# Pinning three engines to the order of the source in an expert loop, with the index work drawn apart

## The chip, the core and the metric

The kernel runs on one core of a Trainium2 chip. The metric is the device time of one execution in microseconds; lower is better.

## What is computed

A decoder layer over 512 tokens of width 1024, in float32: a mixer of retention and differential attention, then an expert network of 32 experts, of which every token takes four, then a last norm. The change touches the expert network alone:

```python
def moe_ffn(h, w_router, b_router, w1, b1, w2, b2):
    ...
    top_v, top_i = lax.top_k(logits, TOP_K)
    gate = jax.nn.softmax(top_v, axis=-1)
    ...
    def expert_block(args):
        xb, e = args
        hid = xb @ w1[e] + b1[e]
        return swiglu_clamped(hid) @ w2[e] + b2[e]
    ...
    out = jax.ops.segment_sum(ys.astype(jnp.float32) * slot_w[:, None], slot_tok, num_segments=T)
```

w1 is 1024 x 2048 and w2 1024 x 1024 an expert: 12 MB of weights for each of 32 experts, all of which are read.

## The kernel before

**Weights.** A matrix product is made of three: each operand is split into a high and a low part in the fast matmul format, and `three()` (L520 to L523) adds high x high (L521), high x low (L522) and low x high (L523). The weights stream from memory in chunks of 1 MB (128 x 2048 floats, two pages of the 48 that `Pages` hands out), eight for w1 and four for w2 of an expert. SyncE issues the loads (L134). `Whole.make` converts a chunk: ScalarE writes the high part to a second pair of pages (L481), VectorE overwrites the raw chunk with the low part (L484); for the first experts GpSimd does some of the latter. When TensorE is through with a chunk, `done()` frees its four pages, `st.pump()` issues the next load into two of them and `cm.run()` converts the next chunk into two, as long as fewer than five converted chunks stand ready (`Whole(5)`). `st.keep` holds back pages; it is 12 from expert 29 on.

**The loop** (L1313 ff.) runs e from 0 to 32. Iteration e does w1 of expert e and then w2 of expert e - 1. `w1_start(e)` (L1109) lays the biases down in PSUM banks 0 to 3 by four matmuls. `w1_unit(e, u)` is one of 16 units of six matmuls; after each odd unit a chunk is done. After unit 2, `turn_hidden` transposes the hidden rows of expert e - 1 (L1099, eight transposes into banks 4 and 5), and ScalarE and VectorE take them out as two parts (L1087, L1088). Then come eight units of w2 into banks 6 and 7, six matmuls each, with a chunk done after each odd one. After unit 0 and unit 1 `swiglu` reads half of banks 0 to 3 (ScalarE L1127, VectorE L1128 and L1129); after unit 2 `turn` transposes the gathered rows of the next expert (L1092, then L1087 and L1088 again). `result(e - 1)` scales the product by the gate on ScalarE (L1205), and GpSimd adds its rows to y in memory by an indirect DMA (L1206).

**The index work.** `index(e)` writes a one-hot of 128 slots x 512 tokens on VectorE (OH, one buffer; L1064), multiplies it with a small table by four matmuls (L1068, bank 4), reads out the row numbers and the gate by three small VectorE instructions (L1069, L1071, L1072), and gathers the expert's rows from memory by GpSimd (L1080) into `Xg[e % 2]`. In iteration e it is called for expert e + 2 after unit 0 of w1. For the last two experts it also transposes the one-hot (L1077).

**The end.** The last two experts aren't scattered: `result_last` (L1150 to L1152) splits their rows, `combine` (L1160) adds them by matmuls, and `gather_sums` (L1168 to L1173), called after expert 29's result, loads the other input of the sum and the rows of y (GpSimd's queue, L1173). `add_sums(i)` (L1176, L1177) multiplies and adds them on VectorE, called after units 4 to 7 of w2 of expert 30. `finish` norms and stores.

**Order.** The source lists the instructions, but Tile's scheduler orders each engine's queue by its own model of when things are ready; data dependences hold in any order. `tc.keep_in_program_order(ins)` ties an instruction behind the one before it on its engine in the source. Before the change this is used in a few places only (`later_dma`, `first_rows`, the first conversions). At run time each engine takes its queue strictly in the order given.

Of the kernel before, what the change touches and what calls it, by code (L numbers as in the profile page):

```python
# [17 lines left out]
ALU = mybir.AluOpType  # L18
AX = mybir.AxisListType

P = 128
D = 1024
S = 512
NT = S // P
KT = D // P
E = 32
# [78 lines left out]
class Stream:  # L105
# [18 lines left out]
    def issue(self):  # L124
        src, n, shape = self.items[self.next]
        if shape is None:
            self.next += 1
            src()
            return
        b = Buf(self.mem, n)  # L130
        v = b.ap
        if len(shape) == 2:
            v = v.rearrange("p (a b) -> p a b", a=shape[0])
        self.nc.sync.dma_start(v, src)  # L134
        self.bufs[self.next] = b
        self.next += 1
# [51 lines left out]
    yield from b  # L188


@with_exitstack
def decoder_layer(ctx, tc, t, out):
    nc = tc.nc
    pe, dve, act, pool = nc.tensor, nc.vector, nc.scalar, nc.gpsimd
    cp = ctx.enter_context(tc.tile_pool(name="cp", bufs=1))
    pp = ctx.enter_context(tc.tile_pool(name="pp", bufs=1, space=bass.MemoryType.PSUM))
    dp = ctx.enter_context(tc.tile_pool(name="dp", bufs=1, space=bass.MemoryType.DRAM))
# [4 lines left out]
    def bank(b, n=1):  # L202
        return ps[:, b * 512:(b + n) * 512]
# [96 lines left out]
    iota1, tri, iota32, sel64 = cst[:, 0:128], cst[:, 128:256], cst[:, 256:288], cst[:, 288:352]  # L300
# [22 lines left out]
    def sm(name, shape, dt=F32):  # L323
        if name not in small:
            small[name] = cp.tile(shape, dt, name=name)
        return small[name]
# [98 lines left out]
    class Conv:  # L425
# [4 lines left out]
        def __init__(self, ahead):  # L430
            self.units, self.made, self.ahead, self.next, self.sub = [], {}, ahead, 0, dve
            self.pinned = False
# [425 lines left out]
    VAL = cp.tile([P, NT, E, 4], F32R, name="VAL")  # L858
    posm = cp.tile([P, NT, E], F32, name="posm")
# [42 lines left out]
    OH = cp.tile([P, NT, P], F32R, name="OH")  # L902
# [158 lines left out]

    def index(e):
        if e > 0:
            dve.tensor_tensor(OH, iota1.unsqueeze(1).to_broadcast([P, NT, P]),  # L1064
                              posm[:, :, e:e + 1].to_broadcast([P, NT, P]), op=ALU.is_equal)
        o = bank(4)[:, 0:4]
        for i in range(NT):
            pe.matmul(o, OH[:, i, :], VAL[:, i, e, :], start=(i == 0), stop=(i == NT - 1))  # L1068
        dve.tensor_tensor(idx[e % 6], o[:, 0:2], spare, op=ALU.add)  # L1069
        gs = sm("gs", [P, 2])  # L1070
        dve.tensor_copy(gs, o[:, 2:4])  # L1071
        dve.tensor_scalar(gate[e % 6], gs[:, 0:1], gs[:, 1:2], 1.0 / ALPHA, op0=ALU.add, op1=ALU.mult)  # L1072
        if e == 0:
            return
        if e >= E - LAST:
            for i in range(NT):
                pe.transpose(bank(5)[:, i * P:(i + 1) * P], OH[:, i, :].bitcast(F32), ident)  # L1077
            oht[e] = Buf(mem, 1).r[:, 0:512]
            act.activation(oht[e], bank(5), AF.Copy)
        pool.indirect_dma_start(out=Xg[e % 2].ap, out_offset=None, in_=h2_dram,  # L1080
                                in_offset=bass.IndirectOffsetOnAxis(ap=idx[e % 6][:, 0:1], axis=0),
                                bounds_check=S - 1, oob_is_err=False)

    def turned(b, hb, lb):
        for n in range(2):
            cs = slice(n * 512, (n + 1) * 512)
            act.activation(hb.r[:, cs], bank(b + n), AF.Copy)  # L1087
            dve.tensor_tensor(lb.r[:, cs], bank(b + n), hb.r[:, cs].bitcast(F32), op=ALU.subtract)  # L1088

    def turn(src, hb, lb):  # L1090
        for k in range(KT):
            pe.transpose(bank(4 + k // 4)[:, (k % 4) * P:(k % 4 + 1) * P], src[:, k * P:(k + 1) * P], ident)  # L1092
        turned(4, hb, lb)
# [12 lines left out]
    def w1_start(e):  # L1106
        for n in range(4):
            h = n // 2
            pe.matmul(bank(n), selr[:, h * E + e:h * E + e + 1].to_broadcast([P, P]),  # L1109
                      b12.r[:, n % 2 * 512:(n % 2 + 1) * 512], start=True, stop=False)  # L1110

    def w1_unit(e, u):
        k = u // 2
        wH, wL = cm.get(u1[e][k])
        xh, xl = parts(XH, XL, k)
        for n in range(2 * (u % 2), 2 * (u % 2) + 2):
            cs = slice(n * 512, (n + 1) * 512)
            three(bank(n), xh, xl, wH[:, cs], wL[:, cs], False, k == KT - 1)
        if u % 2:
            cm.done(u1[e][k])  # L1120
            cm.run()

    def swiglu(n, sg, ub):

        hid = bank(2 * n, 2).rearrange("p (f two) -> p f two", two=2)
        cs = slice(n * 512, (n + 1) * 512)
        act.activation(sg.ap[:, cs], hid[:, :, 0], AF.Silu, scale=ALPHA)  # L1127
        dve.tensor_scalar(ub.ap[:, cs], hid[:, :, 1], -LIMIT + 1.0, LIMIT + 1.0, op0=ALU.max, op1=ALU.min)  # L1128
        dve.scalar_tensor_tensor(sg.ap[:, cs], sg.ap[:, cs], SILU_MAX, ub.ap[:, cs], op0=ALU.min, op1=ALU.mult)  # L1129
# [45 lines left out]
    def add_sums(i):  # L1175
        dve.tensor_tensor(sums[i].ap, sums[i].ap, g2_row, op=ALU.mult)  # L1176
        dve.tensor_tensor(xt[i], xt[i], sums[i].ap, op=ALU.add)  # L1177
        sums[i].free()
# [134 lines left out]
    index(0)  # L1313
    index(1)
    for e in range(E + 1):
        if e < E:
            w1_start(e)
            if e == E - LAST - 1:
                st.keep = 12
            for u in range(16):  # L1320
                if e == 0 and u >= 13:
                    cm.sub = pool
                w1_unit(e, u)
                if u == 2 and e > 0:
                    turn_hidden(aH, aL)
                if u == 0 and e + 2 < E:
                    index(e + 2)
                if e == 0 and u == 3:
                    gates_turned()
                if e == 0 and u in (5, 7, 9, 11):  # L1330
                    first_sums((u - 5) // 2)
        if e > 0:
            for u in range(8):
                w2_unit(e - 1, u)
                if e < E and u in (0, 1):
                    swiglu(u, sg, ub)
                if u == 2 and e + 1 < E:
                    turn(Xg[(e + 1) % 2].ap, XH, XL)
                if u == 4 and e == E - 1:
                    turn_hidden(XH, XL)  # L1340
                if e == E - LAST + 1 and u >= 4:
                    add_sums(u - 4)
            if e - 1 >= E - LAST:
                result_last(e - 1)
            else:
                result(e - 1)
            if e == E - LAST:
                gather_sums()
        else:
            swiglu(0, sg, ub)  # L1350
            swiglu(1, sg, ub)
            count_extra()
            cm.sub = dve
            turn(Xg[1].ap, XH, XL)

    for b in [XH, XL, aH, aL, sg, ub, yb] + Xg:
        b.free()

# [121 lines left out]
```

## Time and profile before

| | us |
|---|---|
| median of 3 runs | 1585.27 (1583.05 to 1587.38) |
| the profiled execution, its own time | 1585.85 |
| its span, first to last instruction | 1584.0 |
| busy: TensorE / VectorE / ScalarE / GpSimd | 1473.3 / 1323.9 / 993.9 / 171.3 |

PE is TensorE, PEld its weight loads, DVE VectorE, ACT ScalarE, POOL GpSimd, SP SyncE. A matmul of 512 columns shows a duration of about 0.39 us, but the next one starts 0.23 us after it: for TensorE the distance from start to start counts. A wait is put down to what came last.

### The profile page before, as it was taken

The page shows a single profiled execution, that of the slowest core. Times are in us where ns is not written, and L with a number is a line of the kernel's source. Part 1 is how long each engine was busy: PE and PEld are TensorE (multiplying, and loading weights), DVE is VectorE, ACT ScalarE, POOL GpSimd, SP SyncE. Part 2 cuts the span into 40 slices and gives each one's busy share as a digit, 9 for nine tenths or more (in the row PEclk, how much of TensorE's full clock was granted, in tenths as well). Part 3 has the DMA queues.
Part 4 walks back from the last instruction along what each step waited for, and adds up shares of the span by engine and source line. Part 5 has one row for each costly group of instructions (what it writes and reads, how often), then busy time and mean ns, then how long its engine had stood idle before and what let it go on. Part 6 is the DMA issues. An engine that isn't in the chain of part 4 may idle for free.

```text
span 1584.0 us, 18643 instructions
## 1 busy us (share of the span) xinstructions
PE 1473.3 (93%) x6837; PEld 1195.5 (75%) x6837; DVE 1323.9 (84%) x1405; ACT 993.9 (63%) x917; POOL 171.3 (11%) x94
## 2 busy tenths in 40 slices
PE   3999999787999999999999999999999999999956
PEld 3787688766888888888777777777777777887744
DVE  6868767996999989888888888888888888888767
ACT  3525434466777777766666666666666666776724
POOL 0000000442000111111000000000000011110001
PEclk9999999988999999999999999999999999999978
DMA  9871473548999999999999999999999999987962
GB/s 364 314 272 30 157 266 134 198 180 312 353 363 363 372 356 358 369 364 359 351 345 346 345 348 334 354 336 342 346 340 339 345 346 349 349 321 277 329 246 81
DMA packets 88812, 485.19 MB, mean 306 GB/s; under 512 B 12433, under 2 KB 18996, under 8 KB 39182
## 3 DMA queue, kind: packets, MB, share of 16 engines
q1 hardware_dynamic: 75792, 453.54, 76.1%
q0 software_dynamic: 9360, 18.05, 4.5%
q10 hardware_dynamic: 3566, 12.37, 2.1%
q8 instruction: 56, 0.92, 0.2%
q14 instruction: 38, 0.31, 0.1%
HBM read 475.82 MB, written 25.44 MB: 316 GB/s over the span
## 4 chain that ended last, share of the span: by engine, by line
PE 58%; DVE 8%; ACT 5%; DMA 5%; issue 2%; POOL 1%; ACTq 0%; DVEq 0%; POOLq 0%
PE ps L522 19%; PE ps L523 18%; PE ps L521 16%; DVE part L484 6%; ACT part L481 5%; DMA page<-in_w_dram 3%; PE ps L1099 2%; PE ps L1092 1%; PE ps L1109 1%; DMA y_dram<-page,idx 1%; POOL part L484 1%; DMA page<-y_dram 1%; DVE page L1129 0%; DVE page L1368 0%; DMA page<-x_dram 0%
## 5 line engine op out<-in xcount | busy, mean ns | idle before, releaser
L484 DVE TENSOR_TENSOR part<-page,part 128x2048 fp32r<-128x2048 f32 x378 | 855.3, 2287 | 98.8 <-ACT part L481 96.6
L481 ACT ACTIVATE part<-page 128x2048 fp32r<-128x2048 f32 x384 | 718.8, 1912 | 80.9 <-PE ps L522 70.7
L522 PE MATMUL ps<-part,part 128*128 128x512 f32 x1792 | 721.6, 403 | 49.2 <-DVE part L484 41.9
L523 PE MATMUL ps<-part,part 128*128 128x512 f32 x1792 | 706.4, 394 | 3.5 <-DVE part L1088 3.5
L521 PE MATMUL ps<-part,part 128*128 128x512 f32 x1792 | 623.3, 396 | 3.3 <-ACT part L616 3.2
L522 PEld LDWEIGHTS ps<-part,part 128*128 128x128 f32 x1792 | 339.6, 190 | 137.4 <-DVE part L484 61.7
L521 PEld LDWEIGHTS ps<-part,part 128*128 128x128 f32 x1792 | 338.9, 189 | 78.4 <-issue 3.7
L523 PEld LDWEIGHTS ps<-part,part 128*128 128x128 f32 x1792 | 339.6, 190 | 73.0 <-DVE part L1088 4.2
L1087 ACT ACTIVATE part<-ps 128x512 fp32r<-128x512 f32 x128 | 74.1, 598 | 170.2 <-PE ps L1099 81.4
L1206 POOL DMA_INDIRECT y_dram<-page,idx x30 | 71.9, 2397 | 740.7 <-ACT page L1205 705.3
L1088 DVE TENSOR_TENSOR part<-ps,part 128x512 fp32r<-128x512 f32 x128 | 86.3, 684 | 38.0 <-ACT part L1087 38.0
L1127 ACT ACTIVATE page<-ps 128x512 f32<-128x512 f32 x64 | 37.6, 589 | 118.8 <-PE ps L523 118.8
L1080 POOL DMA_INDIRECT page<-h_dram,idx x31 | 47.6, 1534 | 282.7 <-DVE gs L1071 270.5
L1128 DVE TENSOR_SCALAR page<-ps 128x512 f32<-128x512 f32 x64 | 43.8, 687 | 22.0 <-ACT page L1127 21.9
L447 ACT ACTIVATE part<-page 128x1024 fp32r<-128x1024 f32 x32 | 33.5, 1055 | 26.4 <-DMA page<-in_w_in_dram 9.3
L450 DVE TENSOR_TENSOR part<-page,part 128x1024 fp32r<-128x1024 f32 x32 | 38.7, 1221 | 10.7 <-ACT part L447 10.5
L1129 DVE SCALAR_TENSOR_TENSOR page<-page,page 128x512 f32<-128x512 f32 x64 | 47.3, 746 | 0.0
L1109 PE MATMUL ps<-part,selr 128*128 128x512 f32 x128 | 40.8, 411 | 5.8 <-DVE page L1128 4.8
L420 DVE SCALAR_TENSOR_TENSOR page<-page,sc,page 128x1024 f32<-128x1024 f32 x32 | 40.9, 1280 | 5.3 <-DMA page<-in_w_ada_dram 4.9
L1099 PEld LDWEIGHTS ps<-ident,page 128*128 128x128 f32 x256 | 40.5, 202 | 5.1
L1205 ACT ACTIVATE page<-ps,gate 128x1024 f32<-128x1024 f32 x30 | 33.5, 1116 | 15.6 <-PE ps L523 15.6
L1099 PE MATMUL ps<-ident,page 128*128 128x128 f32 x256 | 41.8, 279 | 0.0
(219 smaller groups left out, 803.4 us busy)
## 6 DMA issues: line engine op xcount, KB each, us to landing
page<-in_w_dram SPq DMA_DIRECT2D x384, 1024.0 KB
page<-in_w_ada_dram SPq DMA_DIRECT2D x22, 1024.0 KB
page<-in_w_in_dram SPq DMA_DIRECT2D x12, 1024.0 KB
page<-in_w_out_dram SPq DMA_DIRECT2D x4, 1024.0 KB
page<-in_x_dram SPq DMA_DIRECT2D x4, 512.0 KB
page<-in_w_ada_dram SPq DMA_DIRECT2D x4, 512.0 KB
page<-in_x_dram SPq DMA_DIRECT2D x2, 1024.0 KB
x_dram<-page ACTq DMA_DIRECT2D x4, 512.0 KB
```

The lines of the kernel that those rows point to most:

```text
L481: ins = act.activation(h.r, b.ap, AF.Copy)
L484: ins = self.sub.tensor_tensor(b.r, b.ap, h.r.bitcast(F32), op=ALU.subtract)
L521: pe.matmul(o, aH, bH, start=first, stop=False)
L522: pe.matmul(o, aH, bL, start=False, stop=False)
L523: pe.matmul(o, aL, bH, start=False, stop=last)
L1080: pool.indirect_dma_start(out=Xg[e % 2].ap, out_offset=None, in_=h2_dram, in_offset=bass.IndirectOffsetOnAxis(ap=idx[e % 6][:, 0:1], axis= ...
L1087: act.activation(hb.r[:, cs], bank(b + n), AF.Copy)
L1088: dve.tensor_tensor(lb.r[:, cs], bank(b + n), hb.r[:, cs].bitcast(F32), op=ALU.subtract)
L1099: pe.transpose(bank(4 + k // 4)[:, (k % 4) * P:(k % 4 + 1) * P], src[:, k // 2, k % 2, :], ident)
L1109: pe.matmul(bank(n), selr[:, h * E + e:h * E + e + 1].to_broadcast([P, P]), b12.r[:, n % 2 * 512:(n % 2 + 1) * 512], start=True, stop=False)
L1129: dve.scalar_tensor_tensor(sg.ap[:, cs], sg.ap[:, cs], SILU_MAX, ub.ap[:, cs], op0=ALU.min, op1=ALU.mult)
L1206: pool.indirect_dma_start(out=y_dram, out_offset=bass.IndirectOffsetOnAxis(ap=idx[e % 6][:, 1:2], axis=0), in_=yb.ap, in_offset=None, boun ...
```

## The change

The three engines' handles are wrapped, so that each instruction issued through them while `pin` is set is tied behind the one before it on its engine. `pin` is set for TensorE, VectorE and ScalarE from iteration 1 to the end of the loop; GpSimd and SyncE are not wrapped. `index` is cut in three: `place` (the one-hot), `look_up` (the four matmuls) and `take_rows` (the rest). In iterations 1 to 29 `look_up(e + 2)` follows unit 8 of w1, `take_rows(e + 2)` unit 10, and `place(e + 3)` follows unit 0 of w2 and the first half of the SwiGLU. Expert 0's iteration still calls `index(2)` after unit 0, and ends with `place(3)`.

```diff
+class Engine:
+
+    def __init__(self, tc, engine):
+        self.tc, self.engine, self.pin = tc, engine, False
+
+    def __getattr__(self, name):
+        f = getattr(self.engine, name)
+
+        def issue(*args, **kw):
+            ins = f(*args, **kw)
+            return self.tc.keep_in_program_order(ins) if self.pin else ins
+
+        return issue
...
-    pe, dve, act, pool = nc.tensor, nc.vector, nc.scalar, nc.gpsimd
+    pe, dve, act, pool = Engine(tc, nc.tensor), Engine(tc, nc.vector), Engine(tc, nc.scalar), nc.gpsimd
...
     def index(e):
         if e > 0:
-            dve.tensor_tensor(OH, iota1.unsqueeze(1).to_broadcast([P, NT, P]),
-                              posm[:, :, e:e + 1].to_broadcast([P, NT, P]), op=ALU.is_equal)
+            place(e)
+        look_up(e)
+        take_rows(e)
+
+    def place(e):
+        dve.tensor_tensor(OH, iota1.unsqueeze(1).to_broadcast([P, NT, P]),
+                          posm[:, :, e:e + 1].to_broadcast([P, NT, P]), op=ALU.is_equal)
+
+    def look_up(e):
+        for i in range(NT):
+            pe.matmul(bank(4)[:, 0:4], OH[:, i, :], VAL[:, i, e, :], start=(i == 0), stop=(i == NT - 1))
+
+    def take_rows(e):
         o = bank(4)[:, 0:4]
-        for i in range(NT):
-            pe.matmul(o, OH[:, i, :], VAL[:, i, e, :], start=(i == 0), stop=(i == NT - 1))
         dve.tensor_tensor(idx[e % 6], o[:, 0:2], spare, op=ALU.add)
...
     for e in range(E + 1):
+        if e == 1:
+            pe.pin = dve.pin = act.pin = True
...
-                if u == 0 and e + 2 < E:
-                    index(e + 2)
+                if e == 0 and u == 0:
+                    index(2)
+                if 0 < e < E - 2:
+                    if u == 8:
+                        look_up(e + 2)
+                    if u == 10:
+                        take_rows(e + 2)
...
                 if e < E and u in (0, 1):
                     swiglu(u, sg, ub)
+                if u == 0 and e < E - 3:
+                    place(e + 3)
...
             turn(Xg[1].ap, XH, XL)
-
+            place(3)
+
+    pe.pin = dve.pin = act.pin = False
```

## Rows read from the trace of the kernel before

**Rows 1.** The page: its first line, and the granted TensorE clock in 40 slices of the span, in tenths of full speed.

```profile
span 1584.0 us, 18643 instructions
...
PEclk9999999988999999999999999999999999999978
```

**Rows 2.** The windows: stretch, its length, then the busy time (and the count of instructions) of PE, PEld, DVE, ACT and POOL, the granted clock, the DMA share, GB/s.

```profile
405.40:693.50 288.10, 288.10 (x1346) 240.12 (x1345) 257.48 (x191) 212.59 (x150) 31.78 (x16) 1.00 0.97 364
700.00:1400.00 700.00, 679.19 (x3101) 550.49 (x3101) 601.30 (x443) 481.31 (x351) 72.51 (x38) 1.00 0.94 346
949.80:1064.30 114.50, 110.78 (x506) 89.52 (x505) 98.37 (x73) 78.37 (x58) 11.33 (x6) 1.00 0.94 341
```

**Rows 3.** The timeline of GpSimd: the scatters of experts 0, 8, 10 and 29.

```profile
408.55 2.60 POOL L1206 DMA_INDIRECT y_dram<-page,idx  x1 [35.58 <-ACT page L1205]
...
695.05 1.96 POOL L1206 DMA_INDIRECT y_dram<-page,idx  x1 [30.73 <-ACT page L1205]
...
770.92 2.46 POOL L1206 DMA_INDIRECT y_dram<-page,idx  x1 [21.24 <-ACT page L1205]
...
1495.13 2.44 POOL L1206 DMA_INDIRECT y_dram<-page,idx  x1 [35.37 <-DMA page<-x_dram]
```

**Rows 4.** The timeline of TensorE, 512 to 521 us: the first matmul of an expert's w1, the index products, the transposes, the matmul after them.

```profile
514.32 0.39 PE L521 MATMUL ps<-part,part 128*128 128x512 f32 x1
...
515.69 0.50 PE L1068 MATMUL ps<-VAL,OH 128*128 128x4 f32 x4
...
518.93 1.11 PE L1099 MATMUL ps<-ident,page 128*128 128x128 f32 x8
519.79 0.48 PE L521 MATMUL ps<-part,part 128*128 128x512 f32 x1
```

**Rows 5.** Who waited for whom, 441.4 to 549.4 us (three experts): us in total, times, longest. These are the waits of VectorE and of ScalarE's conversions; TensorE has none.

```profile
ACT part L481 <- PE ps L522: 23.9, 33, 1.2
DVE part L484 <- ACT part L481: 9.8, 21, 0.9
```

**Rows 6.** The same view, 949.8 to 1064.3 us (three experts): the waits of TensorE's matmuls.

```profile
PE ps L522 <- DVE part L484: 3.6, 6, 1.0
```

**Rows 7.** The timeline of TensorE, 985 to 997 us: two of the four bias products and what follows them.

```profile
987.95 0.63 PE L1109 MATMUL ps<-part,selr 128*128 128x512 f32 x2
989.53 0.50 PE L522 MATMUL ps<-part,part 128*128 128x512 f32 x1 [0.95 <-DVE part L484]
```

**Rows 8.** Groups of instructions by line and shape, 441.4 to 549.4 us: count, busy us, mean ns of one, idle before.

```profile
L484 DVE TENSOR_TENSOR part<-page,part 128x2048 fp32r<-128x2048 f32 x37 | 84.3, 2290 | 9.8 <-ACT part L481 9.8
L481 ACT ACTIVATE part<-page 128x2048 fp32r<-128x2048 f32 x36 | 69.1, 1921 | 25.7 <-PE ps L522 23.9 <-ACT part L1087 1.8
...
L1088 DVE TENSOR_TENSOR part<-ps,part 128x512 fp32r<-128x512 f32 x12 | 7.9, 678 | 0.0
...
L1087 ACT ACTIVATE part<-ps 128x512 fp32r<-128x512 f32 x12 | 6.5, 596 | 0.9 <-PE ps L1099 0.5
L1128 DVE TENSOR_SCALAR page<-ps 128x512 f32<-128x512 f32 x6 | 4.1, 682 | 0.0
L1129 DVE SCALAR_TENSOR_TENSOR page<-page,page 128x512 f32<-128x512 f32 x6 | 4.1, 681 | 0.0
...
L1064 DVE TENSOR_TENSOR OH<-cst,posm 128x512 fp32r<-128x512 f32 x3 | 2.0, 678 | 0.0
...
L1072 DVE TENSOR_SCALAR gate<-gs 128x1 f32<-128x1 f32 x3 | 0.6, 204 | 0.0
L1069 DVE TENSOR_TENSOR idx<-ps,cst 128x2 uint32<-128x2 f32 x3 | 0.4, 149 | 0.0
```

**Rows 9.** The timeline of all engines, 536 to 553 us: the second half of the SwiGLU on ScalarE and VectorE, the bias products of the next expert, the scatter.

```profile
539.39 0.57 ACT L1127 ACTIVATE page<-ps 128x512 f32<-128x512 f32 x1
...
544.62 0.68 DVE L1128 TENSOR_SCALAR page<-ps 128x512 f32<-128x512 f32 x1
...
549.43 1.09 PE L1109 MATMUL ps<-part,selr 128*128 128x512 f32 x4
...
552.60 2.56 POOL L1206 DMA_INDIRECT y_dram<-page,idx  x1 [32.09 <-ACT page L1205]
```

**Rows 10.** The tail, 1483 us to the end: two of the waits, then three rows of VectorE's timeline.

```profile
PE ps L522 <- DVE part L484: 18.9, 5, 11.0
DVE page L1176 <- DMA page<-y_dram: 11.4, 1, 11.4
...
1520.15 2.35 DVE L1177 TENSOR_TENSOR page<-page,page 128x1024 f32<-128x1024 f32 x2
...
1561.93 1.43 DVE L1150 SCALAR_TENSOR_TENSOR page<-ps,gate,page 128x512 f32<-128x512 f32 x2 [2.18 <-PE ps L523]
1563.38 1.37 DVE L1152 TENSOR_TENSOR part<-page,part 128x512 fp32r<-128x512 f32 x2
```

**Rows 11.** The chain that ended last, 900 to 980 us: two loads of a weight chunk, start and us.

```profile
902.79 6.06 DMA page<-in_w_dram
...
934.29 5.10 DMA page<-in_w_dram
```

**Rows 12.** The timelines of GpSimd and of VectorE between experts 0 and 1.

```profile
357.71 8.98 POOL L484 TENSOR_TENSOR part<-page,part 128x2048 fp32r<-128x2048 f32 x2 [15.59 <-ACT part L481]
...
362.56 5.28 DVE L1129 SCALAR_TENSOR_TENSOR page<-page,page 128x512 f32<-128x512 f32 x2
```

## The prediction

> **What bounds the kernel now.** I read the page for its span and clock [rows 1], then the windows by stretch, then the queue of GpSimd as a clock that ticks once an expert, then TensorE's order in two stretches, and last the waits.
>
> The windows [rows 2] show two regimes inside one loop that does the same work for every expert. From 405.4 to 693.5 us TensorE is busy for all 288.10 us, 36.0 us for each of eight experts. From 700 to 1400 us it is busy for 679 of 700. GpSimd's scatters, one an expert, give the pace [rows 3]: 36.0 us apart up to 695.05 (286.5 us for eight), then from 770.92 to 1495.13 724.2 us for 19, 38.1 us each. So 2.1 us an expert went missing in the middle of the run.
>
> The order of TensorE says where. In the fast stretch it is that of the source: six matmuls of a unit with no hole, 514.32 to 515.69, then four index products, and eight transposes at 518.93 [rows 4]. In the slow stretch the order is another: pairs of the third and second product, the first products ahead, two bias products at 987.95 and then a hole of 0.95 us before a matmul that waits for the low part of the weights [rows 7]. The waits agree: in three experts of the fast stretch TensorE waits for nothing, ScalarE waits for TensorE to free a page, VectorE for ScalarE [rows 5]; in three of the slow one TensorE waits for VectorE's L484 [rows 6]. VectorE's work is the same in both, 257.48 us for eight experts (32.2) and 98.37 for three (32.8) [rows 2]. So the engines have room; in the slow stretch the conversions of the weights come late because they stand late in their queues. The loads are no cause: in the fast stretch no conversion waits for a DMA, though 364 GB/s flow.
>
> The sum is made against the profiled execution: span 1584.0 us, its own time 1585.85, so 1.85 us lie around the span. It is 0.6 us above the median of 1585.27.
>
> **The change, part by part.**
>
> *The pins.* They add no instruction and no wait; they make the three queues follow the source from expert 1 on. Experts 2 to 9 already ran in that order at 36.0 us, so I take 36.0 for all. Lower bound: TensorE has no hole there, so no gain below it. Upper bound: 38.1, the slow pace.
>
> *The index products* (four, 515.69 to the next unit) go from unit 0 to unit 8: the same four, TensorE costs nothing new. The one-hot they read is written an expert's second half earlier, so they don't wait. *Their readers*, L1069, the copy beside it, and L1072, 0.5 us on VectorE [rows 8], go behind unit 10, where VectorE idles between conversions (9.8 us in three experts [rows 5]): nothing. If that cover were gone they would delay a conversion by 0.5 us, and conversions run up to five chunks ahead of TensorE.
>
> *The one-hot* L1064, 0.68 us [rows 8], goes to VectorE between the two halves of the SwiGLU. What waits for that stretch is the next expert's bias product, which needs banks 2 and 3 read out: the second L1128 ends at 545.30, the bias products start at 549.43 [rows 9], 4.1 us of slack. It shrinks to 3.4: nothing. Source order also puts the second ACTIVATE L1127 behind the second conversion instead of ahead (539.39 becomes some 542.2 [rows 9]); L1128 stood behind that conversion's L484 on VectorE anyway: nothing. With the cover gone, each us late would cost an expert 1 us.
>
> *The gather* L1080, on GpSimd's queue, which isn't pinned, is issued some 12 us later in an expert and may change places with the scatter before it (2.6 us [rows 9]). Its rows are read by the transposes of the next expert's second half, over 40 us on: nothing. SyncE's loads keep their number; they are issued when TensorE frees pages, so they speed up with it. *Experts 30 and 31* keep eight extra transposes at about 0.11 us, 0.9 us by their price before [rows 4], and two copies on ScalarE, hidden.
>
> *The middle.* The scatter of expert 0 is at 408.55. With 29 periods of 36.0 and the 0.9 the scatter of expert 29 stands at 408.55 + 1044.0 + 0.9 = 1453.5, against 1495.13: 41.6 us gained.
>
> *The tail.* Before, 88.9 us follow that scatter. In it VectorE waits 11.4 us at L1176 for the rows of y, with conversions queued behind, and TensorE waits 18.9 us for L484 in all [rows 10]. In source order the sums stand behind unit 4 of the last-but-one w2, and y is there long before. I walk this stretch. The bias products of expert 31 come 3.2 us before the scatter (549.43 and 552.60 [rows 9]): 1450.3. Four of them 0.9, sixteen units of 1.37 (514.32 to 515.69), transposes 0.86 and two w2 units bring TensorE to x = 1476.7 [rows 4]. With pages kept back the loads now run one unit ahead: a 1 MB load takes 5.1 to 6.1 us [rows 11], a conversion 1.92 on ScalarE, so VectorE starts the second chunk of the last w2 at about x + 5.1. From there it is the bound, in order: three L484 at 2.29 are 6.9, one L1128 with L1129 1.4, two L1088 1.4, eight sums at 1.18 are 9.4 [rows 8, 10], and two results of two halves, each 0.72 + 0.60 on ScalarE (as L1087) + 0.69 plus hand-overs, 8.7: together 27.8, so x + 32.9 = 1509.6. TensorE ends w2 of the last expert before that, near x + 24, after some 4 us of wait for the second SwiGLU half. The end of the second L1152 group, 1564.75, lay 19.25 us ahead of the end of the span. So 1509.6 + 19.3 = 1528.9, and with 1.85 around it 1530.8: **1531 us**, 41.6 us from the middle and 13.5 from the tail. Bounds of the tail: with no wait at all, 46.5 us of TensorE from 1450.3 and 22.1 from its last w2 matmul to the end, 1518.9, so 1521; if it stays as long as now, 1453.5 + 88.9 + 1.85 = 1544. Before expert 1 nothing is pinned; one more one-hot (0.68 us) stands at the end of expert 0, one index step fewer at the start of expert 1. The order there can shift: I take 0, and 3 us to either side.
>
> **Rule against row.** The fast stretch moves 364 GB/s [rows 2], and conversions there never wait for a load [rows 5]. The Trainium skill, Perfetto Trace Analysis, section Engine Utilization, has 358 GB/s as a core's full share of the memory. By that rule the pace would be 364/358 x 36.0 = 36.6 and the time 1544, an estimate. The trace speaks against it for eight experts, not for thirty; its section Roofline also allows a lone core more.
>
> **Rivals.**
>
> *The loads become the bound* (0.09). The slow stretch moves 346 GB/s [rows 2]; if 364 can't be held over 1100 us, the pace falls back to 364/346 x 36.0 = 37.9, and 21 experts lose 1.9: 1571. For it: DMA share 0.97. Against: that share held for 288 us, and ScalarE's waits name TensorE alone. The skill's 358 above is the mild form of this.
>
> *The order is not the cause, or isn't changed* (0.06). If something else slowed the run at 700 us, or the scheduler still has its way, only part of the tail comes: 1573 to 1586. Against: the waits change with the order.
>
> *VectorE becomes the bound, and it is slower* (0.05). In a pinned queue nothing can pass a late instruction. The place is the second half of an expert, where VectorE runs without a hole up to the second L1088; it decides where VectorE's work per expert passes 36.0 us, and the kernel is slower from about 38.2 on. At 32.2 there are 3.8 us to spare. If L484 took 2.8 instead of 2.29, twelve of them would make 38.3 and each wait on top some 0.5: 29 experts lose 2.8 and the time is 1612. For it: beside GpSimd's own L484 two L1129 took 5.28 us instead of 1.4 [rows 12]. Against: GpSimd does no such work from expert 1 on, and eight experts ran so. The Trainium skill, TensorE: Matmul & The Clock Gate, section Part 1, calls ScalarE's and VectorE's queues strictly first in, first out; the trace agrees, a ready conversion stood 11.4 us behind L1176.
>
> **How the numbers follow.** The forecast has 0.80, with its own range of 1519 to 1547 from the tail's bounds and the start. The range reaches into the milder half of the first rival: 1519 to 1553. A measurement of this kernel tells 0.3%, about 5 us, from no change. Faster: forecast, first rival and a third of the second, 0.91; same 0.04; slower 0.05.
>
> **What would show it.** Right: scatters 36.0 us apart from expert 0 to 29, the last near 1453; TensorE without holes from 405 to 1470; L1176 not waiting for y_dram; VectorE without a hole for the last 30 us before L1152. Wrong: a pace of 36.5 to 38 with ScalarE waiting for a DMA (first rival); TensorE's old pairs past 700 us (second); bias products waiting for L1128, or L484 above 2.5 us (third); or a new wait of TensorE at the index products, which I excluded.

## The result and the profile after

The changed kernel takes 1535.68 us, the median of four runs (1535.39 to 1535.95), against 1585.15 (1583.05 to 1587.38): a ratio of 0.9688, with a 95% interval of 0.9671 to 0.9704. That is 49.5 us less; the forecast was 1531, within 1519 to 1553. The profiled execution took 1535.43 us and has a span of 1533.6.

In the rows that follow, every instruction that goes through the wrapped handles shows the wrapper's line L201. So groups are told by their tiles: part<-page of 128x2048 on ACT and part<-page,part on DVE are the two halves of a conversion (L481 and L484 before), ps<-VAL,OH are the index products, page<-ps of 128x512 is the SwiGLU. On POOL the scatter is L1231 now, the gather L1105.

The page's first line and the granted clock, which answer to [rows 1]:

```profile
span 1533.6 us, 18670 instructions
...
PEclk9999999978999999999999999999999999999988
```

The same three stretches as in [rows 2], by windows (length, busy time of PE, PEld, DVE, ACT, POOL, granted clock, DMA share, GB/s):

```profile
405.40:693.50 288.10, 288.10 (x1346) 240.17 (x1345) 264.09 (x193) 216.64 (x153) 22.48 (x16) 1.00 0.97 363
700.00:1400.00 700.00, 700.00 (x3269) 583.38 (x3268) 640.21 (x468) 526.75 (x370) 54.28 (x39) 1.00 0.97 360
949.80:1064.30 114.50, 114.50 (x537) 95.51 (x537) 105.20 (x77) 86.14 (x62) 8.38 (x6) 1.00 0.97 359
```

The scatters of experts 0, 8, 10 and 29 on GpSimd, which answer to [rows 3]:

```profile
407.61 1.77 POOL L1231 DMA_INDIRECT y_dram<-page,idx  x1 [17.57 <-ACT page L201]
...
695.68 1.73 POOL L1231 DMA_INDIRECT y_dram<-page,idx  x1 [17.59 <-ACT page L201]
...
767.71 1.74 POOL L1231 DMA_INDIRECT y_dram<-page,idx  x1 [17.59 <-ACT page L201]
...
1450.86 2.35 POOL L1231 DMA_INDIRECT y_dram<-page,idx  x1 [32.30 <-ACT page L201]
```

TensorE's waits from 400 us to the end; those of [rows 6] are gone, and all that is left lies in the tail, behind 1478 us:

```profile
PE ps L201 <- DVE page L201: 9.0, 2, 6.6
PE ps L201 <- DVE part L201: 1.0, 1, 1.0
PE ps L201 <- ACT part L201: 0.2, 1, 0.2
```

The second regime is gone. TensorE is busy for 700.00 of 700 us, where it was 679.19; 3269 matmuls fit in instead of 3101. The scatters keep one pace: (767.71 - 407.61) / 10 = 36.0 us, and (1450.86 - 767.71) / 19 = 35.96. Of the 50.4 us between the two spans 44.3 are gained up to expert 29's scatter (1495.13 - 1450.86, of which 0.9 before expert 0's), and 6.1 behind it: 88.9 us before, 82.7 now.

### The profile page after: what moved, and what is told of

Its sections match the earlier page's. It is cut to its first block, busy times and chain, and to the rows that moved or that the text cites. A ratio compares the mean times of both kernels' runs of the same rounds, so it can differ in the third digit from the quotient of the medians.

```text
span 1533.6 us, 18670 instructions
## 1 busy us (share of the span) xinstructions
PE 1455.1 (95%) x6837; PEld 1198.3 (78%) x6837; DVE 1331.5 (87%) x1405; ACT 1012.8 (66%) x917; POOL 139.6 (9%) x94
## 4 chain that ended last, share of the span: by engine, by line
PE 88%; DVE 6%; DMA 2%; ACT 1%; issue 1%; POOL 1%; ACTq 0%; DVEq 0%; POOLq 0%
PE ps L201 88%; DVE page L201 3%; DVE part L201 1%; ACT part L201 1%; DMA page<-in_w_dram 1%; POOL part L500 1%; DMA page<-in_p_b_dram 0%; DMA page<-in_w_ada_dram 0%; DVE rs_a L201 0%; ACT page L201 0%; DMA ident<-in_c_ident_dram 0%; DVE n2s L201 0%; DVE f L201 0%; DVE o L201 0%; ACT L201 0%
## 5 line engine op out<-in xcount | busy, mean ns | idle before, releaser
L201 PE MATMUL ps<-part,part 128*128 128x512 f32 x5416 | 1288.6, 395 | 13.6 <-POOL part L500 5.2
L201 PEld LDWEIGHTS ps<-part,part 128*128 128x128 f32 x5416 | 1012.0, 189 | 232.1 <-DVE part L201 7.0
L201 DVE TENSOR_TENSOR part<-page,part 128x2048 fp32r<-128x2048 f32 (+1 forms) x419 | 905.3, 2183 | 117.3 <-ACT part L201 113.6
L201 ACT ACTIVATE part<-page 128x2048 fp32r<-128x2048 f32 (+1 forms) x425 | 777.0, 1834 | 325.6 <-PE ps L201 241.2
L201 PE MATMUL ps<-ident,page 128*128 128x128 f32 (+1 forms) x652 | 94.9, 286 | 19.8 <-ACT page L201 10.1
L201 ACT ACTIVATE page<-ps 128x512 f32<-128x512 f32 (+5 forms) x121 | 70.5, 588 | 64.4 <-PE ps L201 51.7
L201 PEld LDWEIGHTS ps<-ident,page 128*128 128x128 f32 (+1 forms) x652 | 84.5, 170 | 35.4 <-ACT page L201 18.3
L1231 POOL DMA_INDIRECT y_dram<-page,idx x30 | 55.0, 1832 | 543.1 <-ACT page L201 543.1
L201 ACT ACTIVATE part<-ps 128x512 fp32r<-128x512 f32 (+1 forms) x135 | 73.6, 595 | 35.9 <-PE ps L201 31.9
L201 DVE TENSOR_TENSOR part<-ps,part 128x512 fp32r<-128x512 f32 x132 | 84.8, 683 | 3.9 <-ACT part L201 3.9
L1105 POOL DMA_INDIRECT page<-h_dram,idx x31 | 32.7, 1055 | 469.4 <-DVE gs L201 458.5
L201 DVE SCALAR_TENSOR_TENSOR page<-page,sc,page 128x1024 f32<-128x1024 f32 (+1 forms) x48 | 59.1, 1237 | 5.5 <-DMA page<-in_w_ada_dram 4.6
L201 PE MATMUL ps<-page,page 128*128 128x128 f32 (+4 forms) x304 | 50.0, 328 | 1.3 <-ACT page L201 0.9
L201 DVE SCALAR_TENSOR_TENSOR page<-page,page 128x512 f32<-128x512 f32 x64 | 48.2, 754 | 2.2
L201 DVE TENSOR_SCALAR page<-ps 128x512 f32<-128x512 f32 x64 | 43.7, 684 | 4.7 <-ACT page L201 4.7
L201 PEld LDWEIGHTS ps<-page,page 64*128 64x128 f32 (+1 forms) x304 | 35.9, 188 | 14.2 <-ACT page L201 5.3
L201 PE MATMUL ps<-part,selr 128*128 128x512 f32 x128 | 37.0, 409 | 5.8 <-DVE page L201 4.8
L201 PEld LDWEIGHTS ps<-part,selr 128*128 128x128 f32 x128 | 24.7, 194 | 15.9 <-DVE page L201 5.1
L201 DVE TENSOR_TENSOR OH<-cst,posm 128x512 fp32r<-128x512 f32 x31 | 35.0, 1128 | 0.0
L201 ACT ACTIVATE page<-ps,gate 128x1024 f32<-128x1024 f32 x30 | 33.0, 1100 | 1.6 <-PE ps L201 1.6
L201 ACT ACTIVATE page<-page,da_mx 128x128 f32<-128x128 f32 (+3 forms) x32 | 17.8, 557 | 18.4 <-DVE da_mx L201 18.4
L201 DVE TENSOR_TENSOR page<-ps,page 128x512 f32<-128x512 f32 (+3 forms) x28 | 15.9, 572 | 15.6 <-PE ps L201 15.6
```

What stands on the lines that cost most here:

```text
L201: ins = f(*args, **kw)
L1231: pool.indirect_dma_start(out=y_dram, out_offset=bass.IndirectOffsetOnAxis(ap=idx[e % 6][:, 1:2], axis=0), in_=yb.ap, in_offset=None, boun ...
```

## The experiments

All diffs are against the changed kernel. The pace is the mean distance of the scatters of experts 10 to 26; a ratio is taken to the runs of before made beside that kernel.

| kernel | what is left of the change | pace, us | median, us | ratio to before (95%) |
|---|---|---|---|---|
| before | nothing | 38.1 | 1585 | |
| e1_pins_only | three pins, index work in one piece at unit 0 | 41.2 | 1681.33 | 1.0605 (1.0577 to 1.0633) |
| e2_apart_only | index work apart, no pin | 37.3 | 1570.41 | 0.9907 (0.9885 to 0.9929) |
| e3_pin_pe | apart, TensorE pinned | 37.2 | 1561.52 | 0.9856 (0.9832 to 0.9879) |
| e6_pin_dve | apart, VectorE pinned | 37.7 | 1569.43 | 0.9895 (0.9879 to 0.9912) |
| e7_pin_act | apart, ScalarE pinned | 36.0 | 1544.66 | 0.9740 (0.9724 to 0.9756) |
| e4_pin_dve_act | apart, VectorE and ScalarE pinned | 36.0 | 1534.99 | 0.9684 (0.9663 to 0.9706) |
| e5_place_apart | three pins, only the one-hot apart | 36.5 | 1545.50 | 0.9747 (0.9730 to 0.9763) |
| after | all | 36.0 | 1535.68 | 0.9688 (0.9671 to 0.9704) |

**The pins without the drawing apart.**

```diff
-                if e == 0 and u == 0:
-                    index(2)
-                if 0 < e < E - 2:
-                    if u == 8:
-                        look_up(e + 2)
-                    if u == 10:
-                        take_rows(e + 2)
+                if u == 0 and e + 2 < E:
+                    index(e + 2)
...
-                if u == 0 and e < E - 3:
-                    place(e + 3)
...
-            place(3)
```

> The three engines pinned, but the index work whole and in its old place behind unit 0 of w1. Theory A (the queues' order is the lever, and drawing the index work apart is what makes the pins harmless): in source order the one-hot stands on VectorE behind the conversions of the w2 half, which end some 4 us after TensorE reaches the index products (conversion of the last w2 chunk about 17.7 us after the end of w1, index products wanted at 14.1). TensorE waits 3 to 4.5 us for OH in each of 29 experts: 1620 to 1665 us, slower than the kernel before. Rival B (the pins bring the whole gain, the place of the index work is indifferent): 1536. Rival C (the index work apart brings the gain, the pins none): 1585.

It took 1681.33 us, 98 us more than the runs of before beside it (1583.43) and above the range expected. TensorE's only wait after 400 us (us in total, times, longest):

```profile
PE ps L201 <- DVE OH L201: 91.6, 28, 3.3
```

One of these on TensorE, by the timeline (start, length, what, and in brackets the idle time before it):

```profile
941.75 1.53 PE L201 MATMUL ps<-part,part 128*128 128x512 f32 x6
946.58 0.61 PE L201 MATMUL ps<-VAL,OH 128*128 128x4 f32 x4 [3.29 <-DVE OH L201]
947.05 4.60 PE L201 MATMUL ps<-part,part 128*128 128x512 f32 x12
951.49 1.11 PE L201 MATMUL ps<-ident,page 128*128 128x128 f32 x8
```

What VectorE did meanwhile:

```profile
939.24 6.68 DVE L201 TENSOR_TENSOR part<-page,part 128x2048 fp32r<-128x2048 f32 x3
945.85 0.68 DVE L201 TENSOR_TENSOR OH<-cst,posm 128x512 fp32r<-128x512 f32 x1
```

And the granted clock around it, by windows:

```profile
930.00:946.50 16.50, 13.29 (x63) 10.74 (x61) 16.00 (x13) 11.56 (x10) 2.51 (x1) 1.00 0.88 336
946.50:951.00 4.50, 4.42 (x14) 3.57 (x15) 0.47 (x4) 1.65 (x1) 1.93 (x2) 0.62 0.48 74
951.00:971.00 20.00, 20.00 (x93) 16.70 (x92) 16.57 (x9) 13.73 (x10) 0.00 (x0) 1.00 0.95 343
```

The one-hot stands where the source has it, behind three conversions that fill VectorE from 939.24 to 945.85; the index products behind it hold TensorE for 91.6 / 28 = 3.27 us an expert. What the expectation left out is the second price: after the wait the granted clock is down, a mean of 0.62 for 4.5 us, which is part at 1.2 and part at 2.4 GHz; behind each of the 28 waits the mean of these 4.5 us lies between 0.50 and 0.70. From the first matmul of w1 to the transposes are 9.74 us here (941.75 to 951.49), where the fast stretch of before has 4.61 for the same instructions (514.32 to 518.93 [rows 4]). That is 5.13 us more: 3.29 for the wait, and 1.8 for slower work behind it. The pace of 41.2 is 5.2 us above 36.0. Strict order helps only where the order is good.

**The drawing apart without the pins.**

```diff
-            pe.pin = dve.pin = act.pin = True
+            pass
```

> The index work drawn apart as in the changed kernel, nothing pinned. Theory A: the scheduler orders the queues by its model, conversions drift late as before, the pace goes from 36.0 to about 38 in the middle: 1575 to 1590. Rival B: the same. Rival C: 1536.

It took 1570.41 us, a little better than expected (1575 to 1590). The pace is 36.0 us up to 691 us and 37.3 from 766 on, against 38.1 before: moving the index work gains 0.8 us an expert by itself, and the pins take away the other 1.3. The two parts don't add: alone they are worth -13 and +98 us, together -50.

**Which pin.** The same line, with one or two handles in it: `pe.pin = True` in e3_pin_pe, `dve.pin = act.pin = True` in e4_pin_dve_act, `dve.pin = True` in e6_pin_dve, `act.pin = True` in e7_pin_act.

> Index work apart, TensorE alone pinned; VectorE and ScalarE as the scheduler orders them. If TensorE's own order is what costs (rival D: pairs and first products ahead): 1536. Theory A says the conversions' place on VectorE and ScalarE counts: as far as the scheduler puts them late, TensorE waits for the low part in source order too, 1545 to 1590, with waits of TensorE for part<-page,part on VectorE.

> Index work apart, VectorE and ScalarE pinned, TensorE free. Theory A: conversions are on time, and TensorE finds all operands ready whatever small swaps the scheduler makes: 1534 to 1545. Rival D: TensorE's order alone costs, so 1575 to 1590.

> Index work apart, VectorE alone pinned. Theory A1 (the drift sits on ScalarE, whose evictions and SwiGLU halves that wait for TensorE stand ahead of conversions): VectorE in source order waits for late ScalarE, 1555 to 1575. Theory A2 (the drift sits on VectorE, the fuller of the two): 1534 to 1540.

> Index work apart, ScalarE alone pinned. Theory A1: conversions start on time, and VectorE can only follow: 1535 to 1548. Theory A2: 1555 to 1575.

TensorE's waits from 400 us to the end, first without a pin, then with TensorE pinned, with VectorE pinned, and with ScalarE pinned:

```profile
PE ps L201 <- DVE part L201: 37.6, 25, 11.1
```

```profile
PE ps L201 <- DVE part L201: 24.1, 26, 6.7
```

```profile
PE ps L201 <- DVE page L201: 30.5, 24, 1.4
PE ps L201 <- ACT part L201: 4.5, 3, 3.4
```

```profile
PE ps L201 <- DVE part L201: 14.6, 1, 14.6
PE ps L201 <- DVE page L201: 3.8, 2, 2.9
```

With TensorE alone pinned the conversions still come late (24.1 us in 26 waits), though 9 us are gained over no pin (1561.52 against 1570.41); with VectorE alone TensorE waits about once an expert for the SwiGLU's output instead. With ScalarE alone the pace is 36.0 to the end, and what TensorE still waits (14.6 us at once, and 3.8) lies in the tail.

ScalarE's queue shows what its pin does. Without a pin (e2_apart_only), by the waits from 700 to 1400 us and by the timeline:

```profile
ACT page L201 <- PE ps L201: 82.8, 20, 7.3
```

```profile
973.89 0.60 ACT L201 ACTIVATE page<-ps 128x512 f32<-128x512 f32 x1 [4.19 <-PE ps L201]
...
977.34 5.52 ACT L201 ACTIVATE part<-page 128x2048 fp32r<-128x2048 f32 x3
```

The scheduler puts ScalarE's half of the SwiGLU ahead of conversions. There ScalarE waits 4.19 us for TensorE to finish the banks, and afterwards three conversions run without a hole between them; it is their low parts for which TensorE waits above. ScalarE's waits at page<-ps (SwiGLU or result) make 82.8 us from 700 to 1400 us, 154.2 with TensorE pinned and 153.8 with VectorE pinned; with ScalarE pinned there is none in that stretch.

So the order of ScalarE's queue is what costs the middle of the run: its pin alone restores the pace. (A kernel with the other two engines pinned and ScalarE free was not run.) VectorE's pin is needed for the tail alone: ScalarE and VectorE together are as fast as all three. Beside these two TensorE's pin buys nothing that these runs can tell.

**Only the one-hot apart**, products and readers together at unit 0:

```diff
-                if 0 < e < E - 2:
-                    if u == 8:
-                        look_up(e + 2)
-                    if u == 10:
-                        take_rows(e + 2)
+                if 0 < e < E - 2 and u == 0:
+                    look_up(e + 2)
+                    take_rows(e + 2)
```

> Pinned as in the changed kernel, the one-hot apart (after unit 0 of w2), but index products and their readers together behind unit 0 of w1. Theory A: TensorE no longer waits for the one-hot, but the readers stand on VectorE behind three conversions that run without a hole (in the changed kernel from 907.55 to about 914.2, bias products at 908.58), and the hidden transposes, wanted about 914.0, need bank 4 read out: 0.5 to 0.7 us an expert over 29, so 1550 to 1557. If only the one-hot's place mattered: 1536. If the readers' place cost as much as the one-hot's: over 1600.

It took 1545.50 us, below the 1550 to 1557 expected; the kind of cost is the expected one and its size a little smaller. The early one-hot takes away 4.7 of the 5.2 us by which e1 is slower an expert, and the place of the products the last 0.5. TensorE waits behind the index products for their readers:

```profile
PE ps L201 <- DVE gs L201: 5.4, 26, 0.2
```

That is 0.2 us an expert; its weight loads show another 0.6 us each for the same reader (11.8 us in 20, from 700 to 1400 us), beside other work for a part.

**Are the loads near their bound?** From expert 2 on `three()` is cut to its first two products:

```diff
-            three(bank(n), xh, xl, wH[:, cs], wL[:, cs], False, k == KT - 1)
+            if e < 2:
+                three(bank(n), xh, xl, wH[:, cs], wL[:, cs], False, k == KT - 1)
+            else:
+                pe.matmul(bank(n), xh, wH[:, cs], start=False, stop=False)
+                pe.matmul(bank(n), xh, wL[:, cs], start=False, stop=(k == KT - 1))
...
-            three(bank(w2_bank(e) + n), ah, al, wH[:, cs], wL[:, cs], u == 0, u == KT - 1)
+            if e < 2:
+                three(bank(w2_bank(e) + n), ah, al, wH[:, cs], wL[:, cs], u == 0, u == KT - 1)
+            else:
+                pe.matmul(bank(w2_bank(e) + n), ah, wH[:, cs], start=(u == 0), stop=False)
+                pe.matmul(bank(w2_bank(e) + n), ah, wL[:, cs], start=False, stop=(u == KT - 1))
```

> From expert 2 on the low x high product is left out, a third of TensorE's matmul work (so the output isn't the reference's); everything else, the 12 MB of loads, the conversions, the order, stays. Theory (TensorE sets the pace of 36.0 us, VectorE and the loads have room): TensorE's need falls to about 36.0 - 48 x 0.2275 = 25.1 us an expert, and the pace falls until VectorE is full at 32 to 33.5 us; 30 experts gain 2.5 to 4 us each, so 1430 to 1465, and VectorE then shows no hole; over 380 GB/s flow. Rival (the loads are the bound, or as good as the bound, at 36.0): the pace stays at 35.3 to 36, the rate at 358 to 368 GB/s, ScalarE's conversions wait for DMAs, time 1515 to 1536.

One run took 1462.75 us, at a pace of 33.9 us: with less work for TensorE the pace falls, so TensorE sets the 36.0. The window and two of ScalarE's waits, both from 700 to 1400 us:

```profile
700.00:1400.00 700.00, 589.70 (x2476) 461.16 (x2476) 666.38 (x485) 544.58 (x391) 109.52 (x44) 0.91 0.98 384
```

```profile
ACT part L201 <- DMA page<-in_w_dram: 133.6, 132, 7.5
ACT part L201 <- PE ps L201: 16.5, 10, 2.3
```

384 GB/s flow for 700 us, so the 360 of the changed kernel are no bound. But the room is small, 2.1 us an expert. At 33.9 us VectorE is busy for 95% of the time, the DMA share is 0.98, and ScalarE, which waited for TensorE before, now waits for loads. Which of the two, VectorE or the loads, sets the 33.9 this run doesn't tell.

**The tail.** Four kernels went at the 82.7 us behind expert 29's scatter. e8_tail releases the pages that are held back (`st.keep = 0` behind `gather_sums()`) and draws the sums forward; e10_keep does the first of these alone; e12_no_sums leaves the eight sums out; e11_sums_pool gives them to GpSimd.

```diff
+                if e == E - LAST + 1 and u >= 14:
+                    add_sums(u - 14)
...
-                if e == E - LAST + 1 and u >= 4:
-                    add_sums(u - 4)
+                if e == E - LAST + 1 and u < 2:
+                    add_sums(u + 2)
...
                 gather_sums()
+                st.keep = 0
```

> The changed kernel with another tail: no pages held back after the sums' buffers are taken (loads of the last chunks earlier), and the four sums behind units 14 and 15 of the last w1 and units 0 and 1 of the last-but-one w2. Theory (the tail is VectorE's, whose queue idles 5.9 us behind conversions whose loads come late): up to 6 us less, 1529 to 1533. If VectorE then waits for y instead, or the end hangs on TensorE: 1534 to 1540.

It took 1535.78 us (1532.93 to 1538.56), a ratio of 0.9692 (0.9676 to 0.9708): nothing is gained, and from the last scatter to the end are 83.0 us, where the changed kernel has 82.7. TensorE's waits for the SwiGLU in the tail grew from 9.0 to 12.4 us, since sums now stood ahead of it in VectorE's queue.

> Against the kernel after: the pages held back are released right after the rows of y are asked for (one half of the tail variant tried before; the sums stay where they are). Theory A (the last loads are issued late because pages are held back, and that delays VectorE's last conversions): ScalarE's wait for loads in the tail falls from 14.5 to 8 to 12.5 us, the last L1152 ends 2 to 4 us earlier than at 1514.56, time 1531 to 1534. B (the last conversions are bound by when TensorE frees pages, or by the loads themselves): within 1 us of the kernel after, 1534.5 to 1537. If A holds, moving the sums was what spoilt the earlier variant.

It took 1532.47 us (1531.66 to 1534.33), a ratio of 0.9673 (0.9660 to 0.9686). By what was named for it theory A seems to hold: the time, ScalarE's wait for loads (9.6 us) and the end of the last L1152 (1511.72, 2.8 us earlier) all lie where it puts them. But counted from the last scatter the trace says otherwise. Its first and last scatter, two VectorE instructions and two waits of ScalarE from 1440 us on:

```profile
404.86 1.83 POOL L1231 DMA_INDIRECT y_dram<-page,idx  x1 [17.52 <-ACT page L201]
...
1448.07 2.35 POOL L1231 DMA_INDIRECT y_dram<-page,idx  x1 [32.30 <-DMA page<-in_p_brow_dram]
```

```profile
1484.72 2.28 DVE L201 TENSOR_TENSOR part<-page,part 128x2048 fp32r<-128x2048 f32 x1
...
1511.03 0.69 DVE L201 TENSOR_TENSOR part<-page,part 128x512 fp32r<-128x512 f32 x1 [0.70 <-ACT part L201]
```

```profile
ACT part L201 <- PE ps L201: 10.4, 5, 3.6
ACT part L201 <- DMA page<-in_w_dram: 9.6, 6, 3.4
```

Expert 0's scatter is already 2.75 us early (404.86 against 407.61), and the spans differ by 2.7. From the last scatter to the end of the last L1152 (1511.03 + 0.69) are 63.65 us and to the end of the span 82.8; in the changed kernel 63.70 and 82.7. ScalarE waits 4.9 us less for loads (9.6 against 14.5), yet the L484 of the second chunk of the last w2 stands 36.65 us behind the scatter (36.70 in the changed kernel). So releasing the pages doesn't bring the end closer to the last scatter, as theory B has it, and in the profiles the 3 us lie ahead of expert 0's scatter, in the part that nothing pins: that scatter lies between 404.48 and 408.84 us in the profiles of these kernels. The gain itself is no scatter of single executions, since every run of e10_keep (at most 1534.33) is below every run of the changed kernel (at least 1535.39). That it lies at the start rests on one profile of each. e4's few tenths can't be told from nothing.

```diff
-        dve.tensor_tensor(sums[i].ap, sums[i].ap, g2_row, op=ALU.mult)
-        dve.tensor_tensor(xt[i], xt[i], sums[i].ap, op=ALU.add)
+        pool.tensor_tensor(sums[i].ap, sums[i].ap, g2_row, op=ALU.mult)
+        pool.tensor_tensor(xt[i], xt[i], sums[i].ap, op=ALU.add)
...
-                if e == E - LAST + 1 and u >= 4:
-                    add_sums(u - 4)
...
                 gather_sums()
+                for i in range(NT):
+                    add_sums(i)
```

(e12_no_sums takes out the first two lines of the diff and changes nothing else.)

> Against the kernel after: the eight sums of the tail go from VectorE to GpSimd, right after the rows of y are asked for. Counted from expert 29's scatter to the end of the span, so that the unpinned start (first scatter between 404.5 and 408.8 in the kernels so far) does not matter: 82.7 us in the kernel after. Theory (VectorE, 33 us without a hole, bounds the tail): the sums' 9.75 us leave it; then the second result can't end before TensorE's last w2, near 1503.2 + 4 = 1507.5 instead of 1514.56, so 4 to 7 us less, 75.5 to 79 us. Rival (GpSimd's 19 us of work, 2.35 each, beside the conversions slows VectorE, as the two L1129 of 5.28 us in [rows 12] do): two or more L484 between 1463 and 1486 take 3 to 5 us, and half or all of the gain is lost: 79 to 84 us.

> The eight sums of the tail are left out (the rows of y and the residual are never added, so the output isn't the reference's); nothing else changes. It gives the value of their place without GpSimd's disturbance. If VectorE bounds the tail: 75.5 to 78 us from expert 29's scatter to the end instead of 82.7. If TensorE or the loads bound it: 81 to 83 us.

e11 took 1557.04 us, 0.9825 (0.9810 to 0.9839), and did neither of the two things expected. In it all engines but GpSimd stand still, by windows and by ScalarE's timeline:

```profile
1472.00:1486.00 14.00, 0.00 (x0) 0.00 (x0) 0.00 (x0) 0.00 (x0) 14.00 (x7) 0.50 0.00 0
```

```profile
1492.07 9.12 ACT L201 ACTIVATE part<-page 128x2048 fp32r<-128x2048 f32 x5 [38.16 <-DMA page<-in_w_dram]
```

GpSimd sums from 1468.68 to 1487.10, nothing is loaded from 1472 on, and the first conversion starts 5 us after the last sum. `add_sums` frees the pages of y as it is issued, now ahead of the last loads in the source, so these pages go to the next loads. SyncE's waits from 1430 to 1500 us show that a load then stood behind GpSimd's sum; in the changed kernel no load waits for GpSimd there:

```profile
SPq L134 <- POOL page L1202: 14.7, 1, 14.7
```

e12, in one run of 1532.47 us, has 1450.39 for the last scatter and a span of 1530.7: 80.3 us, between the two ranges expected and 2.4 less than the changed kernel for 9.75 us of VectorE's work. The result of the last expert now waits for TensorE (VectorE), which from the SwiGLU on has no hole (TensorE):

```profile
1507.58 0.75 DVE L201 SCALAR_TENSOR_TENSOR page<-ps,gate,page 128x512 f32<-128x512 f32 x1 [6.68 <-PE ps L201]
```

```profile
1487.27 1.10 PE L201 MATMUL ps<-ident,page 128*128 128x128 f32 x4 [6.71 <-DVE page L201]
...
1491.55 24.26 PE L201 MATMUL ps<-part,part 128*128 128x512 f32 x98
```

So the sums on VectorE are worth 2.4 us, not 9.75; what sets the end is when the two SwiGLU halves come, and behind them both engines are full.

## Why the prediction was right, and where it was off

**The pins, 36.0 for all experts.** Right: 36.0 us from expert 0 to 29, no wait of TensorE up to 1478 us. One reading was loose: the scatters of the fast stretch before are not all 36.0 apart, for 286.5 us make 35.8 each, one distance being 34.45 (588.57 to 623.02). The 36.0 stood on TensorE's busy window as well, and held. The cause is shown more closely than it was forecast: ScalarE's order is what costs the middle.

**The edits at nothing.** Right as costed: TensorE waits neither at the index products nor at the bias products nor for gathered rows, so products, readers, one-hot and gather cost nothing where they now stand. But the prediction treated them as edits to be excused, and e1 shows that they carry the result: with the pins and the old place the kernel is 6% slower. The rival of a pinned queue in which a late instruction holds the others was right in kind; its place was the one-hot's old one at unit 0, not the conversions, and its price 5.2 us an expert (forecast: 2.8).

**The middle.** Forecast 1453.5 for the last scatter, measured 1450.86. Of the 2.6 us 0.9 came before expert 0's scatter; the rest is that the scatter stands closer behind the work it follows. On TensorE itself the forecast was off by little more than that 0.9: the bias products of expert 31 start at 1449.26, forecast 1450.3.

**The tail.** This is the step that was mis-sized. The last stretch of VectorE and of TensorE in the changed kernel, and two rows of ScalarE, by the timelines:

```profile
1477.43 2.29 DVE L201 TENSOR_TENSOR part<-page,part 128x2048 fp32r<-128x2048 f32 x1 [2.19 <-ACT part L201]
1481.20 2.29 DVE L201 TENSOR_TENSOR part<-page,part 128x2048 fp32r<-128x2048 f32 x1 [1.47 <-ACT part L201]
1484.02 2.29 DVE L201 TENSOR_TENSOR part<-page,part 128x2048 fp32r<-128x2048 f32 x1 [0.53 <-ACT part L201]
1486.23 0.68 DVE L201 TENSOR_SCALAR page<-ps 128x512 f32<-128x512 f32 x1
...
1487.56 2.28 DVE L201 TENSOR_TENSOR part<-page,part 128x2048 fp32r<-128x2048 f32 x1
...
1513.87 0.69 DVE L201 TENSOR_TENSOR part<-page,part 128x512 fp32r<-128x512 f32 x1 [0.70 <-ACT part L201]
```

```profile
1479.78 1.43 PE L201 MATMUL ps<-part,part 128*128 128x512 f32 x5 [0.97 <-DVE part L201]
1487.78 1.10 PE L201 MATMUL ps<-ident,page 128*128 128x128 f32 x4 [6.57 <-DVE page L201]
```

```profile
1482.08 1.91 ACT L201 ACTIVATE part<-page 128x2048 fp32r<-128x2048 f32 x1 [0.91 <-DMA page<-in_w_dram]
1483.89 0.58 ACT L201 ACTIVATE page<-ps 128x512 f32<-128x512 f32 x1
```

The walk put the second chunk of the last w2 on VectorE at x + 5.1 = 1481.8; it started at 1487.56, 5.8 us later. From there the walk held: 27.0 us to the end of the last L1152 (1514.56) for 27.8, and 19.0 to the end of the span for 19.25. 5.8 - 0.8 - 0.2 = 4.8, and the forecast missed by 4.7 (1535.7 for 1531). Counted from the last scatter the tail is 7.3 us longer than the walk's 75.4 (1528.9 - 1453.5); the scatter came 2.6 us earlier than forecast, so two errors of opposite sign met in the total. The "some 4 us" of TensorE's wait for the SwiGLU were 9.0 for the same reason. The walk let loads run one unit ahead once pages were held back; by the windows from 1460 to 1480 us the loads then fill the DMA engines:

```profile
1460.00:1470.00 10.00, 10.00 (x45) 8.29 (x45) 5.59 (x3) 5.75 (x3) 2.21 (x4) 1.00 0.99 407
1470.00:1480.00 10.00, 9.03 (x40) 7.17 (x40) 5.88 (x3) 4.58 (x3) 0.00 (x0) 1.00 1.01 413
```

From 1453 us on ten chunks (10.5 MB) and the rows of y (2.1 MB) go through them, 12.6 MB, which at 410 GB/s would take 31 us, to 1484, an estimate: the walk had not counted them as one stream. Conversions come 3.8 us apart there (1477.43 to 1481.20), where a chunk of w1 keeps TensorE for 2.7. In e10, with the pages released, the DMA share is 1.01 as well (414 GB/s from 1467 to 1477 us), and the chunk comes no earlier behind the scatter. The strict order has a price here too: ScalarE waits for a load at seven conversions (14.5 us in all), the last of them at 1482.08, and the last SwiGLU stands behind these. TensorE was through with the SwiGLU's banks near 1473, an estimate (the last 78 matmuls of w1, from 1455.18, at 1.37 us for six [rows 4]), but ScalarE reached it at 1483.89. What an earlier place would gain was not tried. VectorE as the one bound was wrong as well: e12 shows TensorE 2.4 us behind it. But "L1176 not waiting for y" was right, and so was VectorE's full queue ahead of the last L1152: in the 30.5 us from 1484.02 on its only holes are four hand-overs of 0.70.

**The rule on the loads.** The changed kernel moves 359 to 363 GB/s in the windows of the loop, with no conversion waiting for a load from 700 to 1400 us, and e9 moves 384 for 700 us; the first rival, in which the loads become the bound, fell with that. By the Trainium skill's figure of 358 GB/s in Perfetto Trace Analysis, section Engine Utilization, the time would have been 1544, the prediction's estimate; the trace disagrees, by 7% of rate at least for this lone core (384). The Trainium skill's section Roofline on the same page, which leaves a core that is alone more than that share, agrees with the 384.

**What stays open:** why the scheduler's own order keeps the pace of 36.0 up to about 690 us and loses it then, in before as in the three of these kernels whose ScalarE isn't pinned; and the 4 us by which the unpinned start differs among the kernels.

## What to carry to other kernels

A queue that is pinned to the source makes every place in the source a commitment: look first at what stands ahead of each small instruction on its engine, and draw producer, product and reader apart by as much as that takes. Before all engines are pinned, find the one whose order costs: here it was ScalarE, the first link of the conversions. And compare variants from a mark inside the run, such as the last scatter, before a gain of 3 us is put down to the edit: here it lay in another part of the kernel.

## What was not expected of the hardware

In e1 a wait of TensorE of 3.3 us cost 1.8 us more behind it, at a granted clock of 0.62 from 946.5 to 951.0 us (1.00 on both sides). The clock fell so behind each of the 28 waits, while holes of about 1 us an expert before the change left it at 1.00 [rows 2]. A lone core drew 384 GB/s for 700 us and 413 for 10.
